# Sparse attention: the scores of two heads together, second products on half the rows

## The chip, the cores and the metric

The kernel runs on one core of one Trainium2 chip. The metric is the device time of one execution in microseconds (us). TensorE multiplies, VectorE (DVE) and ScalarE (ACT) read its results from PSUM, GpSimd (POOL) works on SBUF alone, and the SyncE queue (SP) issues most of the transfers.

## The reference

A two-layer decoder trunk on 512 tokens of width 1024, in float32. Each layer is half a SwiGLU block, a token mixer, half a SwiGLU block; layer 0 mixes with latent attention, layer 1 with sparse attention of 16 heads in 4 groups. The change is in the second of these. Its core, cut:

```python
o = gates[..., 0:1] * o_cmp + gates[..., 1:2] * o_sel + gates[..., 2:3] * o_win
# o_sel and o_win, for each head:
s = einsum(q_i, k_i) * scale + bias          # bias by distance, causal mask
p = softmax(where(mask, s, NEG))
o = einsum(p, v_i)
```

With 512 tokens, 8 blocks of 64 and 16 blocks chosen, the selected branch attends to all blocks and the window of 512 covers everything, so both branches are causal softmax attention over 512 keys, with keys and values of their own (branch 0: selected, branch 1: window). The four heads of a group share them.

## The kernel before, in words

Numbers are split in a high part, which TensorE multiplies as fp32r, and a low part (the rest). A product of two numbers is a sum of products of parts.

In the sparse mixer the query of a head is one tile `qs[h]` of 128 rows: for an even head, rows 0 to 63 hold the high part of the 64 query dimensions and rows 64 to 127 the low part; for an odd head it is the other way round (`query`, inner `part`). A group's keys are two tiles per branch (`keys`): `k1` holds the high part of the key in both halves of its rows, `k2` the low part in both halves. A score tile is then two products of 128 rows into one PSUM bank: q by `k1` (high by high and low by high), and q by `k2` (high by low and low by low), the second added to the first.

Queries go in blocks of 128, i = 0 to 3, and block i sees (i + 1) x 128 keys. For i = 0 and 1 both branches share a bank (`front2`, 256 and 512 columns); for i = 2 and 3 each branch has its own (`front`, 384 and 512 columns). So a head has six score tiles. The list of tiles goes by pairs of heads, the even head's tile and then the odd head's of the same block and branch:

```python
order = [(1, None), (0, (0, 0))], [(3, None), (2, (1, 0))], [(3, None), (2, (1, 1))]
```

`attend` walks this list. At step t it calls the front of tile t, then the back of tile t - 4, the end of an earlier pair, and other work planned for that step (`todo`: projections of later heads' queries and keys, values, the compressed branch, the output projection). The fronts take a bank of tag S, of which there are two; the compressed branch's scores take one of the same two. `probs` follows: DVE adds the bias and finds the extreme of each row (`softmax_tile`, L661), which frees the bank; ACT takes the exponential (L662); DVE a reciprocal (L1191); POOL multiplies with the gate (L1194). `back` transposes the probabilities on TensorE (L1215), and ACT and DVE split them (L1226, L1227). `end` multiplies with the values (`pv2`, L1240, and L1248 for the compressed branch) and hands on the output. The bias of a head is a tile `th` fetched by the SP queue at its first block (L1200), four buffers, shared with the compressed branch's bias (`cb`).

A planner puts the instructions of each engine in order: by priority and by its own estimate of when each can run. `high_priority` raises a priority, `issue_after(x)` makes instructions of x's engine follow x in the queue.

Of the kernel before, what the change touches and what calls it, by code (L numbers as in the profile page):

```python
# [11 lines left out]
F32 = mybir.dt.float32  # L12
# [6 lines left out]
P = 128  # L19
S = 512  # L20
# [15 lines left out]
BW = 1040  # L36
BOFF = 528
# [14 lines left out]
URGENT = 400  # L52
# [12 lines left out]
class Kern:  # L65
# [865 lines left out]
    def nsa(self, gain_next):  # L931
        nc, tc, a = self.nc, self.tc, self.a
        with ExitStack() as cx:
# [14 lines left out]
            kt = [self.four() for _ in range(2)]  # L948
# [85 lines left out]
            ks, vs, qs, pc, th, bank, pts = {}, {}, [], {}, {}, {}, {}  # L1034

            with tc.tile_pool(name="cmp", bufs=1, reuse_waits="tile") as bp:
                self.chain, self.chained = None, True
                bt = self.bias_table(bp)
# [80 lines left out]
            tp = cx.enter_context(tc.tile_pool(name="nsat", bufs=2, reuse_waits="tile"))  # L1119
# [50 lines left out]
                f()  # L1170
            o32, oh, ol = [None], [], []

            def front(h, br, i):
                g = h // 4
                if i < 2:
                    return front2(h, i)
                k1, k2 = ks[g][br]
                m, qi = (i + 1) * P, slice(i * P, (i + 1) * P)
                sb = self.bank("S", "s")
                nc.tensor.matmul(sb[:, :m], qs[h][:, qi], k1[:, :m], start=True, stop=False)  # L1180
                last = nc.tensor.matmul(sb[:, :m], qs[h][:, qi], k2[:, :m], start=False, stop=True)
                p_sb = tp.tile([P, S], F32, tag="p", bufs=6, name="p")
                probs(h, (br,), i, sb, p_sb)
                return p_sb, last

            def probs(h, brs, i, sb, p_sb):
                st, m, n = self.stat(), (i + 1) * P, len(brs)
                for x in range(n):
                    xs = slice(x * m, x * m + m)
                    self.softmax_tile(sb[:, xs], th[h][:, 0:m][:, ::-1], i, -1.0, p_sb[:, xs], st[:, x : x + 1], st[:, 2 + x : 3 + x])  # L1190
                nc.vector.reciprocal(st[:, 2 : 2 + n], st[:, 2 : 2 + n])  # L1191
                for x, br in enumerate(brs):
                    t, gate = p_sb[:, x * m : x * m + m], gat[:, i, 3 * h + 1 + br : 3 * h + 2 + br]
                    nc.gpsimd.tensor_scalar(t, t, st[:, 2 + x : 3 + x], gate, op0=ALU.mult, op1=ALU.mult)  # L1194

            def front2(h, i):

                if i == 1:
                    th[h] = tp.tile([P, S], F32, tag="th", bufs=4, name="th")
                    nc.sync.dma_start(th[h], bass.AP(tensor=bt.tensor, offset=bt.offset + h * BW + BOFF - 127, ap=[[1, P], [1, S]]))  # L1200
                m, qi = (i + 1) * P, slice(i * P, (i + 1) * P)
                sb = self.bank("S", "s")
                out = sb[:, : 2 * m].rearrange("p (b n) -> p b n", n=m)
                k = kt[h // 4 % 2].rearrange("p (b z n) -> p b z n", b=2, z=2)[:, :, :, :m]
                nc.tensor.matmul(out, qs[h][:, qi], k[:, :, 0, :], start=True, stop=False)
                last = nc.tensor.matmul(out, qs[h][:, qi], k[:, :, 1, :], start=False, stop=True)
                p_sb = tp.tile([P, S], F32, tag="p", bufs=6, name="p")
                probs(h, (0, 1), i, sb, p_sb)
                return p_sb, last

            def back(p_sb, h, br, i):
                n = i + 1 if i > 1 else 2 * (i + 1)
# [97 lines left out]
            for h in range(0, H, 2):  # L1310
                for br, part in zip((0, 0, 1), order):
                    for i, z in part:
                        for e in range(2):
                            tiles.append((partial(front, h + e, br, i), partial(back, h=h + e, br=br, i=i),
                                          partial(end, h, *z) if z and e else None))
# [121 lines left out]
```

## Time and profile before

| | |
|---|---|
| median of 3 runs | 1862.23 us (1862.03 to 1864.34) |
| profiled execution | 1861.77 us |
| its span, first to last instruction | 1860.0 us |
| granted TensorE clock | 0.999 |
| the sparse mixer's tiles (first score product to last) | about 1283 to 1485 us |
| PE / DVE / ACT / POOL busy over the span | 99 / 83 / 58 / 13% |

Busy PE means that a matmul is under way. Matmuls are pipelined, so the time that one costs is read from its start to the start of the next, not from its length. A weight load (PEld) is the loading of the stationary operand ahead of each matmul, and runs beside the matmul before it. Idle time of an engine that nobody waits for costs nothing.

### The profile page before, as it was taken

What the parts mean: (1) busy time and instruction counts of PE and PEld (TensorE: products, weight loads), DVE (VectorE), ACT (ScalarE), POOL (GpSimd) and SP (SyncE); (2) the same over time, 40 slices, a digit from 0 to 9 for tenths busy, and PEclk for the clock granted to TensorE, in tenths of its full rate; (3) what the DMA queues carried; (4) which work ended last, traced back from release to release, by engine and by line L of the source; (5) the groups of instructions that cost most, each with busy time, mean ns of one, the idle gap of its engine ahead of it and who ended that gap; (6) DMA issues with size and microseconds to landing.
All of it is one profiled execution on the core that took longest, in us unless ns stands there. A gap on an engine that the chain in (4) does not pass through costs nothing. (4 is left out here: it accounts for less than half of the span.)

```text
span 1860.0 us, 32734 instructions
## 1 busy us (share of the span) xinstructions
PE 1841.1 (99%) x12440; PEld 1679.9 (90%) x12440; DVE 1542.0 (83%) x2862; ACT 1083.9 (58%) x2044; POOL 232.9 (13%) x323
## 2 busy tenths in 40 slices
PE   8999999999999999999999999999999999999998
PEld 8999999888889999998999999888888889999997
DVE  8988886688789888887998888765988989988885
ACT  8545554479776554555654545435887866544554
POOL 0000000046500000000000000015666600000000
PEclk9999999999999999999999999999999999999999
DMA  6333333142342333323233332333221124333321
GB/s 245 130 103 102 103 97 115 49 106 72 94 134 94 103 105 112 112 88 115 91 116 110 103 107 87 96 100 97 63 74 63 44 104 131 107 103 106 102 80 67
DMA packets 77901, 187.44 MB, mean 101 GB/s; under 512 B 9632, under 2 KB 37664, under 8 KB 77744
## 3 DMA queue, kind: packets, MB, share of 16 engines
q1 hardware_dynamic: 74640, 180.32, 30.3%
q10 hardware_dynamic: 3104, 5.03, 0.8%
q8 instruction: 98, 1.61, 0.3%
q14 instruction: 59, 0.48, 0.1%
HBM read 178.17 MB, written 2.16 MB: 97 GB/s over the span
## 5 line engine op out<-in xcount | busy, mean ns | idle before, releaser
L167 PE MATMUL pd<-al,wd 128*128 128x512 f32 x576 | 224.1, 389 | 0.0
L168 PE MATMUL pd<-ah,wd 128*128 128x512 f32 x576 | 224.0, 389 | 0.0
L166 PE MATMUL pd<-ah,wd 128*128 128x512 f32 x576 | 224.0, 389 | 0.0
L361 PE MATMUL px<-four,wh 128*128 128x256 f32 x632 | 175.2, 277 | 0.5 <-ACT pg L493 0.5
L363 PE MATMUL px<-four,wl 128*128 128x256 f32 x632 | 174.5, 276 | 0.0
L362 PE MATMUL px<-four,wh 128*128 128x256 f32 x632 | 174.5, 276 | 0.0
L362 PE MATMUL pq<-four,wh 128*128 128x256 f32 x632 | 174.5, 276 | 0.0
L363 PE MATMUL pq<-four,wl 128*128 128x256 f32 x632 | 174.4, 276 | 0.0
L361 PE MATMUL pq<-four,wh 128*128 128x256 f32 x632 | 174.4, 276 | 0.0
L174 ACT ACTIVATE wd<-wdr 128x384 fp32r<-128x384 f32 x192 | 99.2, 519 | 101.5 <-issue 75.5
L175 DVE TENSOR_TENSOR wl<-s,wh 128x512 fp32r<-128x512 f32 x79 | 54.6, 691 | 121.0 <-ACT wh L174 120.9
L413 DVE SCALAR_TENSOR_TENSOR h<-pd,h 128x512 f32<-128x512 f32 x216 | 148.5, 688 | 6.1 <-PE pd L168 6.1
L174 ACT ACTIVATE wh<-s 128x512 fp32r<-128x512 f32 x79 | 49.8, 630 | 136.5 <-PE px L362 131.2
L168 PEld LDWEIGHTS pd<-ah,wd 128*128 128x128 f32 x576 | 108.2, 188 | 22.5
L166 PEld LDWEIGHTS pd<-ah,wd 128*128 128x128 f32 x576 | 108.1, 188 | 19.4
L167 PEld LDWEIGHTS pd<-al,wd 128*128 128x128 f32 x576 | 108.0, 188 | 19.5
L361 PEld LDWEIGHTS px<-four,wh 128*128 128x128 f32 x632 | 118.6, 188 | 1.6 <-ACT pg L493 1.3
L362 PEld LDWEIGHTS px<-four,wh 128*128 128x128 f32 x632 | 118.6, 188 | 0.0
L363 PEld LDWEIGHTS pq<-four,wl 128*128 128x128 f32 x632 | 118.6, 188 | 0.0
L363 PEld LDWEIGHTS px<-four,wl 128*128 128x128 f32 x632 | 118.6, 188 | 0.0
L362 PEld LDWEIGHTS pq<-four,wh 128*128 128x128 f32 x632 | 118.6, 188 | 0.0
L361 PEld LDWEIGHTS pq<-four,wh 128*128 128x128 f32 x632 | 118.6, 188 | 0.0
(367 smaller groups left out, 6037.5 us busy)
## 6 DMA issues: line engine op xcount, KB each, us to landing
wr<-in_w_gu SPq DMA_DIRECT2D x93, 512.0 KB, 3.2
ru<-in_w_gu SPq DMA_DIRECT2D x79, 512.0 KB, 4.2
wdr<-in_w_down SPq DMA_DIRECT2D x192, 192.0 KB, 2.5
wdr<-in_w_down SPq DMA_DIRECT2D x24, 256.0 KB, 2.9
wr<-in_mla_w_o SPq DMA_DIRECT2D x8, 512.0 KB, 3.5
wr<-in_nsa_w_q SPq DMA_DIRECT2D x8, 512.0 KB, 3.5
th<-btab_d SPq DMA_DIRECT2D x16, 256.0 KB, 3.3
wr<-in_nsa_w_o SPq DMA_DIRECT2D x8, 512.0 KB, 3.6
```

The costliest lines, as they stand in the source:

```text
L166: mm(out, wh, xh, start=first, stop=False)
L167: mm(out, wh, xl, start=False, stop=False)
L168: return mm(out, wl, xh, start=False, stop=last)
L174: nc.scalar.activation(hi, src, AF.Copy)
L175: (nc.gpsimd if pool else nc.vector).tensor_tensor(lo, src, f32v(hi), op=ALU.subtract)
L361: mm(out, wh[:, p], xh, start=first and p == 0, stop=False, skip_group_check=True)
L362: mm(out, wh[:, p], xl, start=False, stop=False, skip_group_check=True)
L363: mm(out, wl[:, p], xh, start=False, stop=last and p == KP - 1, skip_group_check=True)
L413: nc.vector.scalar_tensor_tensor(self.h[c], p, 0.5, self.h[c], op0=ALU.mult, op1=ALU.add)
```

## The change

The front of an even head now makes the score tiles of both heads of the pair, and the front of the odd head only takes its tile from `pair`. Two S banks are taken. The first products of both heads (q by `k1`, 128 rows) are issued, one after the other; then the second products, each on the 64 rows that hold the head's high part: rows 0 to 63 of q and `k2` for the even head, 64 to 127 for the odd head. The product of low by low parts is left out. Both second products are bound to follow the odd head's first product on TensorE and have a raised priority, so that one follows directly on the other. The bias tiles of both heads are fetched one after the other at the pair's first tile. `front2` becomes part of `front`; `probs`, `back` and `end` are as before, and the walk over the tiles too.

```diff
             def front(h, br, i):
-                g = h // 4
+                if h % 2:
+                    return pair.pop((br, i))
+                g, m, qi = h // 4, (i + 1) * P, slice(i * P, (i + 1) * P)
                 if i < 2:
-                    return front2(h, i)
-                k1, k2 = ks[g][br]
...
-                sb = self.bank("S", "s")
-                nc.tensor.matmul(sb[:, :m], qs[h][:, qi], k1[:, :m], start=True, stop=False)
-                last = nc.tensor.matmul(sb[:, :m], qs[h][:, qi], k2[:, :m], start=False, stop=True)
...
+                    k = kt[g % 2].rearrange("p (b z n) -> p b z n", b=2, z=2)[:, :, :, :m]
+                    k1, k2, brs = k[:, :, 0, :], k[:, :, 1, :], (0, 1)
+                else:
+                    k1, k2 = [t[:, :m] for t in ks[g][br]]
+                    brs = br,
+                if i == 1:
+                    for e in range(2):
+                        th[h + e] = tp.tile([P, S], F32, tag="th", bufs=4, name="th")
+                        nc.sync.dma_start(th[h + e], ...)
+                sbs = [self.bank("S", "s") for _ in range(2)]
+                outs = ...
+                for e in range(2):
+                    first = nc.tensor.matmul(outs[e], qs[h + e][:, qi], k1, start=True, stop=False)
+                for e in range(2):
+                    es = slice(64 * e, 64 * e + 64)
+                    with self.tc.issue_after(first.ins), self.tc.high_priority(URGENT):
+                        last = nc.tensor.matmul(outs[e], qs[h + e][es, qi], k2[es], start=False, stop=True)
+                both = []
+                for e in range(2):
+                    p_sb = tp.tile([P, S], F32, tag="p", bufs=6, name="p")
+                    probs(h + e, brs, i, sbs[e], p_sb)
+                    both.append((p_sb, last))
+                pair[br, i] = both[1]
+                return both[0]
```

More of the change, by code (lines that the diff above doesn't have):

```diff
@@ L1171, in nsa @@
             o32, oh, ol = [None], [], []
+            pair = {}
             def front(h, br, i):
-                g = h // 4
+                if h % 2:
+                    return pair.pop((br, i))
+                g, m, qi = h // 4, (i + 1) * P, slice(i * P, (i + 1) * P)
                 if i < 2:
-                    return front2(h, i)
-                k1, k2 = ks[g][br]
-                m, qi = (i + 1) * P, slice(i * P, (i + 1) * P)
-                sb = self.bank("S", "s")
[L1180 to L1184, printed above, removed]
+                    k = kt[g % 2].rearrange("p (b z n) -> p b z n", b=2, z=2)[:, :, :, :m]
[6 more added lines that the diff above has]
+                        th[h + e] = tp.tile([P, S], F32, tag="th", bufs=4, name="th")
+                        nc.sync.dma_start(th[h + e], bass.AP(tensor=bt.tensor, offset=bt.offset + (h + e) * BW + BOFF - 127, ap=[[1, P], [1, S]]))
+                sbs = [self.bank("S", "s") for _ in range(2)]
+                outs = [sb[:, :m] if i > 1 else sb[:, : 2 * m].rearrange("p (b n) -> p b n", n=m) for sb in sbs]
+                for e in range(2):
[11 more added lines that the diff above has]
+                return both[0]
             def probs(h, brs, i, sb, p_sb):
@@ L1194, in probs @@
                     nc.gpsimd.tensor_scalar(t, t, st[:, 2 + x : 3 + x], gate, op0=ALU.mult, op1=ALU.mult)
[L1196 to L1209, printed above, removed]
             def back(p_sb, h, br, i):
```

## The prediction

> **What bounds the kernel now.** I read the page first, then the stretch in which the changed lines run (1291 to 1486 us), cut into four windows, then the waits of that stretch. The page's busy line (PE 99%) and its chain (nearly all of what it names is PE) say that TensorE carries the whole kernel; the windows say whether that holds where the change is.
>
> ```profile
> PE 1841.1 (99%) x12440; PEld 1679.9 (90%) x12440; DVE 1542.0 (83%) x2862; ACT 1083.9 (58%) x2044; POOL 232.9 (13%) x323
> ...
> PE 34%; DVE 2%; ACT 0%; issue 0%; POOL 0%; ACTq 0%
> ```
>
> Windows (width, then busy us of PE, weight loads, DVE, ACT, POOL):
>
> ```profile
> 1291.00:1336.00 45.00, 43.96 (x247) 35.12 (x246) 42.83 (x136) 40.47 (x107) 30.24 (x42) 1.00 0.24 78
> 1336.00:1376.00 40.00, 40.00 (x249) 35.35 (x248) 35.58 (x101) 32.45 (x85) 24.92 (x32) 1.00 0.20 61
> 1376.00:1432.00 56.00, 56.00 (x319) 47.83 (x318) 49.00 (x142) 45.49 (x112) 38.90 (x46) 1.00 0.21 67
> 1432.00:1486.00 54.00, 53.92 (x314) 45.81 (x312) 49.76 (x160) 45.93 (x121) 31.32 (x43) 1.00 0.14 45
> ```
>
> In the last three windows PE never rests (40.00 of 40, 56.00 of 56, 53.92 of 54), and DVE has 89, 88 and 92%. In the first one DVE has 42.83 of 45, 95%, and PE has gaps. So time taken from PE shortens the last three windows until DVE is in the way, and little of the first. The waits of the weight loads from 1291 to 1486 (us in all, times, longest) say what PE's gaps hang on:
>
> ```profile
> PEld s L1180 <- DVE small L661: 1.5, 4, 0.6
> PEld ptc L1158 <- POOL e L1153: 0.9, 1, 0.9
> PEld o L1248 <- ACT npt L1226: 0.8, 2, 0.5
> ```
>
> The first row is a score bank that DVE has not yet read, 0.375 us a time; all four lie before 1336. No row has PE waiting for a weight slab.
>
> **What the change removes: array time.** The second score product of a head uses 128 rows now and 64 after, and two heads' second products follow each other on different rows. How many there are, by form:
>
> ```profile
> L1181 PE MATMUL s<-four x44: 335/365/400, 1292.4 to 1485.0; 128*128 128x512 f32 x22, 128*128 128x384 f32 x22
> L1181 PE MATMUL s<-four,q x20: 337/368/403, 1313.1 to 1482.7; 128*128 128x512 f32 x10, 128*128 128x384 f32 x10
> L1206 PE MATMUL s<-four x22: 278/340/399, 1283.4 to 1472.8; 128*128 128x512 f32 x11, 128*128 128x256 f32 x11
> L1206 PE MATMUL s<-four,q x10: 280/338/398, 1305.6 to 1469.3; 128*128 128x512 f32 x5, 128*128 128x256 f32 x5
> ```
>
> Of 512 columns there are 22+10+11+5 = 48, of 384 32, of 256 16: 24, 16 and 8 pairs. What one costs is not its 0.28 to 0.40 us, since products are pipelined, but the step from its start to the next one's. Timeline, first column start, second length:
>
> ```profile
> 1428.02 0.40 PE L1181 MATMUL s<-four 128*128 128x512 f32 x1
> 1428.02 0.59 PEld L1215 LDWEIGHTS pt<-ident,p 128*128 128x128 f32 x4
> 1428.26 0.60 PE L1215 MATMUL pt<-ident,p 128*128 128x128 f32 x4
> ...
> 1434.39 0.34 PE L1181 MATMUL s<-four 128*128 128x384 f32 x1
> 1434.57 0.38 PE L1215 MATMUL pt<-ident,p 128*128 128x128 f32 x2
> ...
> 1422.14 0.28 PE L1206 MATMUL s<-four 128*128 128x256 f32 x1
> 1422.26 0.38 PE L1215 MATMUL pt<-ident,p 128*128 128x128 f32 x2
> ```
>
> So 0.235 us for 512 columns (mostly 0.23), 0.175 for 384, 0.115 for 256. If the second of a pair were free, the gain would be 24 x 0.23 + 16 x 0.175 + 8 x 0.115 = 5.5 + 2.8 + 0.9 = **9.2 us**: the upper end. If the two ran one after the other as now, it is **0**: the lower end of this term, apart from a cost of changing the rows in use (below).
>
> Between them stand the weight loads, which the change does not reduce: still four for a pair. The four transposes above take 0.60 us with 0.27 for one (two last 0.38), so one follows another every 0.11: a load of 128 columns goes in no faster, and the step after a 512-column product hides two of them (0.22 of 0.23). If both heads' half loads go in while the pair's last 128-row product streams, a 512 pair saves 0.23, a 384 pair 0.175 - (0.22 - 0.175) = 0.13, a 256 pair 0.115 - (0.22 - 0.115) = 0.01: 5.5 + 2.1 + 0.1 = **7.7 us**, the value I take, because loads here already run in the shadow of the product before. If the second load starts only once the first head's half product runs, it saves 0.12, 0.065 and 0.005 a pair: 2.9 + 1.0 = **3.9 us**, a rival.
>
> No row of this kernel has 64 rows or two products at once; the nearest is a change of column count between neighbours:
>
> ```profile
> 344.13 0.39 PE L719 MATMUL pr<-x,w 128*128 128x512 f32 x1
> 344.36 0.39 PE L720 MATMUL pr<-x,w 128*64 128x512 f32 x1
> 344.59 0.39 PE L719 MATMUL pr<-x,w 128*128 128x512 f32 x1
> ```
>
> Steps of 0.23, as without a change of shape: I take nothing for changing shape. Bounds: below, 0; above, the array running empty twice a pair, 0.39 - 0.23 = 0.16 us each, 48 x 2 x 0.16 = 15.4 us. The Trainium skill says the opposite of my choice: "TensorEngine Tiling (Array Packing)", Key Properties, states that a change of the tiling mode drains TensorE. By that rule the 15.4 us would be paid and the change would lose; the row above disagrees for columns, and no run here shows it for rows. For the gain the skill is kinder than my sum: "TensorE: Matmul & The Clock Gate", Part 3, gives tiles on different rows about 4 ns between starts; by that the term would be nearly the whole 9.2 us.
>
> **Where it passes to the end.** First products by stretch (L1180, then L1205, in the first window and in the last; count in brackets):
>
> ```profile
> 1291.00:1336.00 45.00, 6.66 (x16) 3.00 (x16) 1.00 0.24 78
> 1280.00:1291.00 11.00, 1.16 (x3) 0.64 (x4) 1.00 0.57 164
> 1291.00:1336.00 45.00, 2.84 (x8) 1.42 (x8) 1.00 0.24 78
> ...
> 1432.00:1486.00 54.00, 8.72 (x22) 4.15 (x22) 1.00 0.14 45
> 1432.00:1486.00 54.00, 3.11 (x8) 1.50 (x8) 1.00 0.14 45
> ```
>
> Of 96, 16 + 8 + 4 = 28 lie before 1336, where DVE sets the pace: their share, 7.7 x 28/96 = 2.2 us, I count as lost. The other 5.5 us come out of 150 us in which DVE is busy 35.58 + 49.00 + 49.76 = 134.3: it goes from 89.6% to 134.3/144.5 = 93%, under the 95% that it reaches before 1336. So 5.5 pass.
>
> **What it adds: both score banks at once.** There are two S banks. Now a head's front takes one while DVE reads the other. After, the first product of head two sits directly behind that of head one, so the pair waits until DVE has read both:
>
> ```profile
> 1301.02 0.08 DVE L661 DVE_READ_ACCUMULATOR2_ANT small<- 128x1 f32 x1
> 1301.16 0.19 PEld L1180 LDWEIGHTS s<-four 128*128 128x128 f32 x1 [0.26 <-DVE small L661]
> 1301.69 0.68 DVE L661 CUSTOM_DVE_ANT_0 p<-s,th 128x512 f32<-128x512 f32 x1
> 1302.29 0.09 DVE L661 DVE_READ_ACCUMULATOR2_ANT small<- 128x1 f32 x1
> ```
>
> This is such a wait now: bank read, 0.14 us later the load. Queued behind a waiting first product are the two half products, the transposes of the tile four back, the value products and the projections; ACT, DVE and POOL then wait for those. Bounds: below, -1.2 us (all of DVE's present waits for scores, next fence, gone, since head two's score comes earlier); above, a full read of 0.68 + 0.09 = 0.77 at each of 48 pairs, 37 us. The planner may put the pair later and the projections and value products before it, some 3 us of PE work per pair (195/48 = 4.1 less the fronts), so I take the low end: in the last window, whose DVE load is near that of the first, waits as often as there, 22 + 8 = 30 of the 96 fronts against 24, 5 x 0.375 = 1.9, half of it: **1.0 us**. In the first window they are in the 2.2 already.
>
> Edits with one answer: the bias tile of head two is fetched next to that of head one, one tile (some 2 us) earlier. SP's queue already stands still for these:
>
> ```profile
> DVE p L661 <- PE s L1181: 1.2, 3, 0.5
> ...
> SPq L1200 <- DVE small L1191: 23.1, 4, 11.8
> ```
>
> Up to 2 us more at each of 8 pairs delays the weight slabs queued behind; free as long as PE waits for no slab, and it would cost those 2 us where one came late. The fronts' softmax, POOL and ACT work keep their number and sizes. The back of tile t-4 is now queued behind four products instead of two, 0.46 us, inside the four tiles of lead.
>
> **Sum.** The profiled execution took 1861.77 us (span 1860.0 and 1.77 around it), 0.46 under the median 1862.23. -5.5 + 1.0 = -4.5 gives 1857.27 there, **1857.7 us** as a median, 0.24% less. The measurement can tell 0.2%, 3.7 us, from no change: faster is below 1858.5, slower above 1866.0.
>
> **Rivals.**
> - *Loads one at a time.* 3.9 us freed, 71% passes (2.8), less 1.0: 1860.4, no change. For: a load starts at its forerunner's start, not earlier (1428.02 in both rows above). Against: those all use the same 128 rows. 0.18.
> - *Not side by side.* Halves stream in turn, nothing freed, the coupling costs its 1.0: 1863.2, no change. For: no row shows two at once. 0.12.
> - *PE waits for the second bank* (slower). Place: the first product of head two, where DVE is fullest (28 + 30 fronts, 29 pairs); price 0.375 each, 10.9 in place of the 1.0, against 5.5: 1862.2 + 5.4 = 1867.6. It decides from 5.5/29 = 0.19 us a wait. For: DVE at 92 to 95%. Against: 4 waits now in 24 fronts. 0.14.
> - *Change of rows empties the array* (the drain). 15.4 against 7.7 freed: +7.7, 1869.9. For: nothing in the trace; against: L719/L720. 0.08.
>
> **How the numbers follow.** The forecast has 0.48, own range 1854 to 1860. Faster 0.48; same 0.18 + 0.12 = 0.30; slower 0.14 + 0.08 = 0.22. Leaving out the drain and the case that all 9.2 us and more pass (1853.0), the range is 1853.0 to 1867.6.
>
> **What would show it.** Right: second products listed with 64*128, their starts within a pair far closer than 0.23 us for 512 columns; the stage from 1291 to 1486 shorter by 4 to 5 us; DVE's share there near 93% and the gain in the last three windows. Wrong: steps of 0.23 between half products (not side by side), 0.11 (loads one at a time), a step over 0.3 before or after a pair (drain); PEld waits for L661 rising from 1.5 to over 7 us (bank); DVE over 95% after 1336, the array time freed turning into PE's waits.

## Result and the profile after

The change makes the kernel slower: 1872.68 us (1871.53 to 1873.66, 5 runs) against 1862.51 (1862.03 to 1864.34, 5 runs), ratio 1.0052, interval 1.0037 to 1.0066. The forecast was 1857.7. The profiled execution has a span of 1869.7 us, 9.7 more than before.

Page of the changed kernel, busy line; then its windows (width, busy us of PE, weight loads, DVE, ACT, POOL):

```profile
PE 1848.8 (99%) x12440; PEld 1671.9 (89%) x12440; DVE 1539.7 (82%) x2862; ACT 1083.6 (58%) x2044; POOL 232.8 (12%) x323
```

```profile
1291.00:1336.00 45.00, 43.32 (x232) 31.66 (x232) 40.26 (x135) 38.05 (x101) 30.24 (x40) 1.00 0.24 73
1336.00:1376.00 40.00, 39.92 (x238) 32.23 (x237) 34.64 (x110) 33.93 (x89) 25.59 (x33) 1.00 0.22 62
1376.00:1432.00 56.00, 56.00 (x322) 44.94 (x321) 47.48 (x137) 43.81 (x109) 36.08 (x44) 1.00 0.19 63
1432.00:1486.00 54.00, 53.91 (x296) 40.89 (x295) 46.35 (x147) 40.53 (x108) 28.80 (x41) 1.00 0.17 54
```

PE looks as busy as before, and DVE is less busy (92% before, 86% now in the last window). So DVE did not become the bound: PE does the same number of products more slowly. That PE reads as busy is the trap here: a product that waits for its weights counts as under way, and so does the one before it, whose recorded length is longer than the step to the next start. The last transpose of the mixer tells where the 9.7 us are, first before, then after (count, min/median/max ns, first and last start):

```profile
L1215 PE MATMUL pt<-ident,p x320: 270/272/306, 1296.0 to 1490.5; 128*128 128x128 f32 x160
```

```profile
L1220 PE MATMUL pt<-ident,p x320: 270/273/331, 1298.9 to 1499.3; 128*128 128x128 f32 x160
```

8.8 of them have come by then, and at most 0.5 of these before the stage (the first score product starts at 1283.1 before, at 1283.6 after). What the weight loads waited for there (changed kernel, 1280 to 1500 us; L1193 are the first products, L1197 the second, L1220 the transposes):

```profile
PEld s L1197 <- issue: 13.1, 44, 0.4
PEld pt L1220 <- issue: 7.6, 34, 0.4
...
PEld s L1193 <- DVE small L661: 1.4, 5, 0.4
```

"issue" is a wait for nothing that the profile shows as a semaphore. It stands 44 times ahead of a load of 64 rows and 34 times ahead of the transposes, which are the first 128-row products behind 42 of the 48 pairs. The loads' wait for a score bank (L661) is 1.4 us, as before (1.5), but PE's own row for it, below first before, then after, has grown: there is one long wait at the start of the stage, behind the first pair, where the load's idle time is put down to "issue".

```profile
PE s L1180 <- DVE small L661: 0.2, 1, 0.2
```

```profile
PE s L1193 <- DVE small L661: 1.6, 2, 1.3
```

The second products themselves:

```profile
L1197 PE MATMUL s<-four x66: 379/466/502, 1289.4 to 1491.5; 64*128 64x512 f32 x33, 64*128 64x384 f32 x22, 64*128 64x256 f32 x11
L1197 PE MATMUL s<-four,q x30: 379/468/500, 1309.6 to 1491.5; 64*128 64x512 f32 x15, 64*128 64x384 f32 x10, 64*128 64x256 f32 x5
```

All 96 run on 64 rows, and one is longer than before (median 0.466 us against 0.365 of L1181). One pair on the timeline:

```profile
1391.25 0.49 PE L1193 MATMUL s<-four 128*128 128x512 f32 x1
1391.67 0.49 PE L1197 MATMUL s<-four,q 64*128 64x512 f32 x1
1391.67 0.49 PE L1197 MATMUL s<-four 64*128 64x512 f32 x1
1392.10 0.66 PE L1220 MATMUL pt<-ident,p 128*128 128x128 f32 x4
```

```profile
1391.67 0.18 PEld L1197 LDWEIGHTS s<-four,q 64*128 64x128 f32 x1 [0.24 <-issue]
1391.67 0.18 PEld L1197 LDWEIGHTS s<-four 64*128 64x128 f32 x1
1392.10 0.42 PEld L1220 LDWEIGHTS pt<-ident,p 128*128 128x128 f32 x4 [0.24 <-issue]
```

The two half products start together, and so do their loads: the change does what it says. But no load goes in ahead of a change of rows. Before, a load started with its forerunner's product and was hidden by it; here it starts only with its own product, 0.42 us after the start of the product before, of which streaming 512 columns takes 0.23. This pair is dearer than most: its first product began with a load that had waited for a score bank and lasts 0.49 instead of 0.40, so 0.09 of the 0.42 comes from that wait. Over all 48 pairs the median step into the halves is 0.09 to 0.10 longer than a step without a change, and the step out of them 0.20.

**Theory A** from this: each stretch of 64-row products costs a fixed price, worked out from the changed kernel's starts as 0.35 us, so about 17 us for 48, against 9.2 saved. **Theory B**: the loss comes from both score banks being held at once and from the order of instructions that follows.

### The profile page after: what moved, and what is told of

It is laid out like the page before. It is cut to its first block, busy times and chain, and to the rows that moved or that the text cites. A ratio compares the mean times of both kernels' runs of the same rounds, so it can differ in the third digit from the quotient of the medians.

```text
span 1869.7 us, 32752 instructions
## 1 busy us (share of the span) xinstructions
PE 1848.8 (99%) x12440; PEld 1671.9 (89%) x12440; DVE 1539.7 (82%) x2862; ACT 1083.6 (58%) x2044; POOL 232.8 (12%) x323
```

## Experiments

Times are medians beside the kernel before on the same chip: 1863.58 us for the first four kernels, 1863.8 for the last three.

**The same order, full rows.** An edit of one line; the traces have every engine's instructions in the order of the changed kernel:

```diff
-                    es = slice(64 * e, 64 * e + 64)
+                    es = slice(0, P)
```

> The changed kernel with the same order of instructions on every engine, but the second products on all 128 rows again, so nothing changes its rows and nothing runs side by side. Theory A (each stretch of 64-row products costs TensorE a fixed 0.35 us, worked out from the changed kernel's trace, 17.0 us over 48 pairs, against 9.2 us saved): 7.8 us less than the changed kernel, about 1865. Theory B (the pair's hold on both score banks, and the order that follows from it, costs the time): no less than the changed kernel, 1873 or, without the 9.2 us saved, up to 1882.

Measured: 1865.55, ratio 1.0011 (1.0002 to 1.002). Against the 1.0052 of the changed kernel that is 0.0041, 7.6 us (4.5 to 10.8 by the two intervals). That is Theory A's number; the pair's banks and the new order together cost 2.0 us, not 10. The "issue" waits ahead of L1197 are gone from its waits:

```profile
PEld s L1193 <- issue: 2.5, 4, 1.8
PEld s L1193 <- DVE small L661: 1.4, 6, 0.3
PEld pt L1220 <- POOL p L1214: 1.1, 2, 0.6
PEld pt L1220 <- issue: 1.0, 4, 0.4
```

**Half rows for one head of the pair.**

```diff
+                    es = slice(0, P) if e else slice(0, 64)
```

> The same order again; of each pair only the even head's second product runs on 64 rows, the odd head's on 128, so the rows change as often as in the changed kernel and no two products run side by side. Theory A: full_rows + 48 x 0.35 = full_rows + 17, about 1882. Theory B: as full_rows, within 2 us.

Measured: 1881.54, ratio 1.0096 (1.0083 to 1.011): full_rows + 16.0, 0.333 us a stretch. With nothing side by side the loss is larger than that of the changed kernel: 1.0096 - 1.0052 = 0.0044, 8.2 us (4.5 to 11.9 by the two intervals), beside the 9.2 worked out as saved. So the saving was there, and was spent. One stretch of 256 columns on its timeline:

```profile
1400.41 0.28 PE L1193 MATMUL s<-four 128*128 128x256 f32 x1
1400.62 0.38 PE L1197 MATMUL s<-four,q 64*128 64x256 f32 x1
1400.93 0.39 PE L1197 MATMUL s<-four 128*128 128x256 f32 x1
1401.15 0.49 PE L1220 MATMUL pt<-ident,p 128*128 128x128 f32 x3
```

The steps are 0.21, 0.31 and 0.22 instead of 0.115: 0.10 into the half, 0.20 out of it, and 0.11 because the 128-row product behind waits for its own load. That is 0.40 a stretch, 19 us for 48, of which 16.0 came. So 2.4 of the 8.2 us (48 x 0.05) would be this dearer stretch, and the saving is measured only roughly, in line with 9.2 within the noise. Since the order is the same, the two traces can be laid beside each other product by product: one_half is 0.1 us behind full_rows at 1280 us, 2.9 at 1336 (13 stretches), 15.1 at 1486 (48 stretches) and 15.2 at the end. The delay grows only where there are stretches, about 0.2 each before 1336 and 0.35 each after it.

**96 rows instead of 64.**

```diff
+                    es = slice(0, P) if e else slice(0, 96)
```

> As one_half, but the even head's second product on 96 rows instead of 64 (its low by low part kept for half the dimensions). Theory A1 (any count of rows but 128 counts as a change): as one_half, about 1882. Theory A2 (only a change between the array as a whole and its half counts, and 96 rows run as the whole array): as full_rows, about 1865. Theory B: as full_rows as well.

Measured: 1865.64, ratio 1.001 (1.0001 to 1.002), as full_rows. The trace has the 96 rows, in steps as of full products (0.46 us for the two first and 0.47 for the two second ones; the second row below stands for the 96-row product and the odd head's 128-row one together):

```profile
1383.13 0.63 PE L1193 MATMUL s<-four 128*128 128x512 f32 x2
1383.59 0.63 PE L1197 MATMUL s<-four 96*128 96x512 f32 x2
1384.06 0.60 PE L1220 MATMUL pt<-ident,p 128*128 128x128 f32 x4
```

So it is not any change in the number of rows that costs, and A2 holds: the price is for going between the whole array and its halves. Other counts than 64 and 96 were not run.

**Half rows without pairs.** The kernel before, its own order, one bank per front:

```diff
-                last = nc.tensor.matmul(sb[:, :m], qs[h][:, qi], k2[:, :m], start=False, stop=True)
+                es = slice(64 * (h % 2), 64 * (h % 2) + 64)
+                last = nc.tensor.matmul(sb[:, :m], qs[h][es, qi], k2[es, :m], start=False, stop=True)
```

(and the same in `front2`).

> The kernel before, with its own order and one front per head, each second product on 64 rows by itself: 96 stretches of 64 rows, no pair, no bank held longer. Theory A: 1862.5 + 96 x 0.35 = 1896. Theory B: as before, 1862.5.

Measured: 1891.53, ratio 1.0153 (1.0139 to 1.0167): +28.0 us, 0.29 a stretch, against 34 expected. Theory B falls as the cause of the loss: there is no pair here, no bank held longer, every engine's order is that of the kernel before, and the loss is the largest of the kernels near the old order. That a stretch costs less than 0.35 fits PE's old waits, which later products no longer meet: the waits of the weight loads over the stage come to 8.4 us before and, apart from the "issue" rows of the halves (L1182, L1208) and of the transposes (L1217), to 3.5 here, and the rows of L661 ahead of fronts (1.5 us before) are gone. That is some 5 of the 6 us. (The profiled run is the slowest of the four, 1895.15, but from 1280 to 1486 us it falls 29 us behind the kernel before, about as much as the median does.) Its timeline shows the price by itself:

```profile
1394.49 0.40 PE L1180 MATMUL s<-four 128*128 128x512 f32 x1
1394.82 0.49 PE L1182 MATMUL s<-four 64*128 64x512 f32 x1
1395.24 0.66 PE L1217 MATMUL pt<-ident,p 128*128 128x128 f32 x4
```

The step into the half is 0.33 instead of 0.23 (0.10, which I read as the array emptying; no row shows that by itself). The half product lasts 0.49 instead of 0.40 (it waits 0.09 for its own load), and the step out of it is 0.42 instead of 0.23: that 0.09 and another 0.10, read the same way. The four transposes take 0.66 instead of 0.60 (their first load, 0.06). 0.10 + 0.09 + 0.10 + 0.06 = 0.35 us, for 64-row products alone as for two side by side.

**Half rows only where they save most.**

```diff
+                    es = slice(64 * e, 64 * e + 64) if i in (1, 3) else slice(0, P)
```

> The changed kernel, with half rows only in the 24 pairs of 512 columns, where the halves side by side save most; the other 24 pairs have full rows. A fixed price of 0.35 us a stretch: full_rows + 24 x (0.35 - 0.23) = full_rows + 3.0, about 1868.5. If the price were to grow with the columns, the loss of the changed kernel over full_rows (7.1 us) would lie mostly here: about 1871.

Measured: 1869.06, ratio 1.0028 (1.0018 to 1.0038). Over full_rows 0.0017 in ratios, 3.2 us: 3.2 / 24 + 0.23 = 0.36 us a stretch (0.26 to 0.47 by the two intervals). These times alone are a weak test, 1869.06 between 1868.5 and 1871. The traces decide: 0.10 into the half and 0.20 out of it at 256 columns in one_half, 0.10 and 0.19 at 512 in the kernel without pairs. The price does not grow with the columns.

**Two pairs in one stretch.** The fronts of two blocks and two heads are made together, four first products and then four second ones, the second block's banks of tag T, with 8 buffers for the probabilities; only the rows of the second products differ between the two kernels (quad_full and quad_half):

```diff
+                for b, tag in zip(blocks, "ST"):
...
+                    for e in range(2):
+                        sb = self.bank(tag, "s")
...
+                for b, e, sb, out, k1, k2, brs, qi in work:
+                    first = nc.tensor.matmul(out, qs[h + e][:, qi], k1, start=True, stop=False)
+                for b, e, sb, out, k1, k2, brs, qi in work:
+                    es = slice(64 * e, 64 * e + 64)   # quad_half; slice(0, P) in quad_full
```

> Control for quad_half: the fronts of two blocks and two heads together, four score tiles, two of them in banks of tag T, with eight buffers for the probabilities and nine for the row statistics; second products on 128 rows. Four banks are held at once, so the coupling is harder than in the changed kernel: 1865 to 1875 by both theories.

> As quad_full, with the four second products on 64 rows, two by two side by side, in one stretch: 24 stretches instead of 48, the same 9.2 us to save. A price for each stretch: 24 x 0.35 = 8.5 against 9.2, so quad_full - 0.7, no difference that can be measured. A price for each product or pair on half rows: quad_full + 7 to 8, as the changed kernel against full_rows.

Measured: 1910.34 and 1911.64, ratios 1.0247 (1.0233 to 1.0261) and 1.0254 (1.024 to 1.0268). Between them 1.3 us, no difference that these intervals can tell: as a price for each stretch asks for, and not the 7 to 8 of a price for each pair. As a time it is weak evidence: quad_full missed its own forecast by more than 35 us, PE is no longer the bound early in the stage, and waits can hide a price:

```profile
1291.00:1380.00 89.00, 81.26 (x447) 67.28 (x446) 62.19 (x182) 59.91 (x150) 54.14 (x74) 1.00 0.27 78
1380.00:1480.00 100.00, 97.80 (x564) 83.14 (x563) 81.11 (x247) 74.73 (x189) 59.43 (x73) 0.98 0.21 64
```

PE has 81.26 of 89. This way of holding four banks costs 46 us, more than putting more work into a stretch could give back; which of the banks, the buffers and the new order costs it was not separated. One stretch of quad_half is the better witness:

```profile
1382.25 0.34 PE L1199 MATMUL s<-four,q 128*128 128x384 f32 x1
1382.52 0.49 PE L1203 MATMUL s<-four 64*128 64x512 f32 x1
1382.52 0.67 PE L1203 MATMUL s<-four,q 64*128 64x384 f32 x2
1382.85 0.34 PE L1203 MATMUL s<-four 64*128 64x384 f32 x1
1383.13 0.33 PE L1224 MATMUL pt<-ident,p 128*128 128x128 f32 x1
```

Four half products, two of 512 and two of 384 columns, take 0.61 us to the next product of 128 rows. Streaming them two by two takes 0.23 + 0.175 = 0.40, so the step out is 0.21 dearer and the step in (0.27 instead of 0.175) 0.10: a price for the stretch, as for one pair. No kernel tried is faster than the one before.

## Why the prediction was wrong

- **The step that failed: "I take nothing for changing shape".** It rested on L719/L720, where the number of columns alternates at steps of 0.23 us. That row says nothing of rows. The price is 0.35 us a stretch by the timeline, 0.29 to 0.36 by the kernels. 48 x 0.35 = 16.8 us in place of 0, which turns -9.2 into +7.6, what full_rows and the changed kernel differ by. The sign named for it, a step over 0.3 before or after a pair, is what the trace shows.
- **The upper bound of that step was too low**, 15.4 us: it counted the array running empty twice, at 0.16 us each. What I read as emptying costs 0.10 each way; the bound left out the loads that no product then hides, 0.15 a stretch. So the rival "change of rows empties the array", with 0.08 and left out of the range, named the mechanism. Its 1869.9 lies within the noise of the 1872.7 (1869.4 to 1874.8), but partly by luck: it set 15.4 against 7.7, where the runs show 16.8 and 2.0 for the banks and the order against 9.2. The "TensorEngine Tiling (Array Packing)" page of the Trainium skill, section Key Properties, was the statement against me: a change of tiling mode drains TensorE. The runs agree for 64 rows against 128; the 96 rows of rows_96 and the 64 columns of L720 cost nothing, so not every smaller shape cost something here.
- **The saving** was under-sized, 7.7 against 9.2: I took loads to queue for one another, but those of the two halves go in together (both at 1391.67). Both rivals that doubted it (loads one at a time, not side by side) are out. The 4 ns between tiles on different rows in the Trainium skill's "TensorE: Matmul & The Clock Gate", Part 3, fit: the two products of a pair start 3 to 4 ns apart in all 48 pairs. one_half measures the saving only roughly (8.2, of which 2.4 would be its dearer stretch).
- **The score banks** were sized at 1.0; pairs and the new order cost 2.0 us (0.4 to 3.7 by full_rows' interval). PE's own waits for a bank (L661) grew from 0.2 us to 1.9 in full_rows and 1.6 in the changed kernel, most of it one wait of 1.3 to 1.4 at the start of the stage. So the hold on both banks is the likely source of most of the 2.0, not in the last window, where the 1.0 was counted, but at the second pair, before the first transposes. No run separates it from the new order.
- **What passes to the end** held in kind: in one_half a stretch before 1336 delayed the later products by 0.2 us of its 0.40, one after 1336 by 0.35. The forecast counted nothing before 1336 and everything after it.

## What to carry to other kernels

Two products on different halves of the rows did run at once here, but each visit to the halves from a stream of whole-array products cost 0.35 us, more than one pair of 512 columns saves (0.23). Count visits, not products: by these numbers a visit has to hold two or more such pairs to pay, which no run here showed, and then the PSUM banks to hold their results are the next price. And a bound for an untried resource is only as good as its nearest row: an alternation of columns was no witness for rows, and an emptied pipeline also uncovers the load behind it.

## What the runs showed of the hardware

Loads for the two halves of the rows went in together, and both products of a pair started 3 to 4 ns apart. 96 rows ran in the steps of 128. Entering and leaving the halves cost 0.10 us each beyond the streaming, read as an emptying array, and the loads on either side, 0.09 and 0.06 us, were uncovered; the steps into and out of the halves were the same for 256, 384 and 512 columns.
